# Down projection of a SwiGLU encoder: two feature chunks per PSUM bank instead of one

## Chip, cores, metric

One NeuronCore of one Trainium2 chip; the seven others do nothing. The metric is device time in microseconds (us) of one execution of the whole kernel. Inputs, outputs and weights lie in HBM in fp32.

## What is computed

Two requests, 1024 and 512 tokens of width 1024, go through the same trunk of two layers. Layer 0 mixes tokens with a Fourier transform, layer 1 with grouped-query attention; after each mixer stands a dense SwiGLU block, whose third product is what the change touches.

```python
D_MODEL, DEPTH, SEQ, DEC_SEQ = 1024, 2, 1024, 512
D_FF = 2816                                     # 22 chunks of 128 features

def swiglu_ffn(x, g, w_gate, w_up, w_down):
    h = rms_norm(x, g)
    return (jax.nn.silu(h @ w_gate) * (h @ w_up)) @ w_down

def run_trunk(x):
    for i in range(DEPTH):
        x = x + (fourier_mixer(...) if i % 2 == 0 else attention_mixer(...))
        x = x + swiglu_ffn(x, norm_ffn[i], ffn_w_gate[i], ffn_w_up[i], ffn_w_down[i])
    return x
```

## The kernel before

Activations are kept with features on the 128 partitions and tokens along the free dimension, in blocks of 512 tokens: block 0 is the short request, blocks 1 and 2 the long one. A width of 1024 is eight chunks (`NC = 8`), the hidden width is 22 chunks (`NF = 22`). Every fp32 operand is split into a high part in `float32r` and a low remainder (`split`: ScalarE copies the high part, VectorE or GpSimd subtracts), and one fp32 product is three matmuls high·high, high·low, low·high with 512 columns, issued by `mm3` (lines 255, 256, 257). "Product" below means one such group of three.

**Two kinds of SwiGLU block.** `ffn` handles block 0 alone. For each hidden chunk `fc` it runs eight products into the gate bank and eight into the up bank (`part`), then SiLU (line 804), the multiplication by up (805), and the split into the tile `mid`; in layer 0 both banks are first multiplied by a row factor (802, 803). `ffn_pair` handles blocks 1 and 2 together, two hidden chunks `f0`, `f1` per pass, by seven steps named B11, B21, T2, T1, B22, T3, N4 in place of eight (a Strassen–Winograd scheme). A step is four quarters `j` of two products each, into two banks; `times` runs it. The stationary operand of a step is put together by `stationary` (ScalarE copy at line 248, GpSimd subtraction at 249, twice each), after GpSimd sums of raw weights in `operands` (lines 966 to 972). The moving operands come from HBM (tiles `ring`) or stay in SBUF (`op`, `late`). A pass yields four `mid` tiles, one for each block and hidden chunk: after B21 (block 1, f0), B22 (block 2, f0), T3 (block 2, f1) and N4 (block 1, f1).

**Down.** Each `mid` tile is multiplied with eight 128x128 pieces of the down weights, one for each output chunk `dc`. Each of these products has a PSUM bank of its own out of two (`bank()`, tag `cF`), and VectorE adds the bank to the fp32 accumulator `acc[dc]` (line 762 in `ffn`, line 900 in `ffn_pair`). So each hidden chunk of each block costs eight products and eight additions.

**What sets the order.** Down products don't follow their `mid` tile at once. They are put on a list `pend`, and taken from it one at a time between the gate and up products: `one()` in `ffn`, at gate chunk 5, 6, 7 and after each up chunk; `some()` in `ffn_pair`, after every one of the 56 products of a pass, with a credit of 0.62. Main stages and side stages (Fourier mixer of the long request, attention, output projections) are generators that `weave` takes turns with, by the costs that they yield and the fixed costs `FFN_US`, `PAIR_US` and so on. The program's scheduler then assigns buffers and may bring an instruction forward on its queue when its buffer is free. SyncE issues the weight loads.

**Buffers.** `weights(src)` loads one 128x1024 piece into one of two `raw` tiles by one DMA, ScalarE copies the high part (line 286) and GpSimd subtracts (line 287) into one of four `w` tiles (tag `wF`). Gate, up, down and the steps' stationary operands all take their `w` tile from these four. There are two `mid` tiles.

The order of the stages: Fourier mixer of block 0; `ffn(0, 0)` woven with the long request's Fourier mixer and with `moving`, which makes the moving operands of the first pair on VectorE (lines 831 to 858); the pair of layer 0 woven with attention of block 0; `ffn(1, 0)` woven with attention of blocks 1 and 2 and with `moving` for the second pair; the pair of layer 1, alone from about 2450 us on.

Of the kernel before, what the change touches and what calls it, by code (L numbers as in the profile page):

```python
# [11 lines left out]
F32R = mybir.dt.float32r  # L12
# [113 lines left out]
def trunk_kernel(ctx: ExitStack, tc: tile.TileContext, t: dict):  # L126
# [18 lines left out]
    for name, kw in (("sbH", {}), ("sbF", {}), ("sbX", {}), ("psF", PS), ("psX", PS)):  # L145
# [10 lines left out]
    }  # L156
    uid = [0]

# [113 lines left out]
    def after(dst, src):  # L272

        dve.tensor_copy(dst[0:1, 0:1], src[0:1, 0:1])

    def weights(src):

        return list(weights_by(src))[-1]

    def weights_by(src):  # L280
        raw = raw_tile(D)
        sp.dma_start(raw, src)
        w = w_tile(2, NC, P)
        yield w
        flat = w.rearrange("p h c n -> p h (c n)")
        pinned(act.copy(flat[:, 0], raw)) if early else act.copy(flat[:, 0], raw)  # L286
        pool.tensor_tensor(flat[:, 1], raw, flat[:, 0].bitcast(F32), op=ALU.subtract)  # L287
        yield w
# [389 lines left out]
    def mixer_projection(seq, done):  # L678
# [8 lines left out]
        for n in range(NC):  # L687
            if two:
                for m in range(len(ws), min(n + 2, NC)):
                    ws.append(weights(cwd[m // 4][:, m % 4].rearrange("p k j c -> p (k j c)")))  # L690
                w = ws[n].rearrange("p h (k j) c -> p h k j c", k=2)
                wv = lambda b, k, j: w[:, b, k, j]
            else:
                wv = lambda b, k, j: turned[n // 4 * 4 + j][:, b, k, n % 4 * P : (n % 4 + 1) * P]
                if n >= 5:
                    early.append(weights_by((t["gate"], t["up"], t["down"])[n - 5][0, 0]))
                    first[n - 5] = next(early[-1])
                if n >= 6:
                    next(early[n - 6])
# [50 lines left out]
    def ffn(layer, b, h, out=None):  # L750
        h = h()
        here = b in resident
        acc = resident.pop(b) if here else accumulators()
        kept[b] = acc
        yield 0.0

        def down(m, wd, fc, dc):
            ps = bank()
            mm3(ps, wd[:, 0, dc], wd[:, 1, dc], m[:, 0], m[:, 1], True, True)
            if fc == 0 and not here:  # L760
                sp.dma_start(acc[dc], xres[b][:, dc, :])
            dve.tensor_tensor(acc[dc], ps, acc[dc], op=ALU.add)  # L762
            if fc == NF - 1:
                new_residual(b, dc, acc[dc], None if out is None else out[:, dc, :])

        def one():
            if pend:
                pend.pop(0)()

        ready = {(v, 0): first[i] for i, v in enumerate(("gate", "up", "down"))} if here else {}  # L770

        def want(v, fc):
            if fc < NF and (v, fc) not in ready:
                ready[v, fc] = weights(t[v][layer, fc])

        for fc in range(NF):
            want("gate", fc)
            want("up", fc)
            want("gate", fc + 1)
            wg, wu = ready.pop(("gate", fc)), ready.pop(("up", fc))  # L780
            ga, up = bankg(), bankg()
            for dc in range(NC):
                part(wg, h, ga, dc)
                if here and fc == 0:
                    part(wu, h, up, dc)
                if dc >= 5:
                    one()
                if dc % 2:
                    yield 1.4 if dc < 5 else 2.4
            want("down", fc)  # L790
            wd = ready.pop(("down", fc))
            for dc in range(NC):
                if dc == 4:
                    want("up", fc + 1)
                if not (here and fc == 0):
                    part(wu, h, up, dc)
                one()
                if dc % 2:
                    yield 2.4 if dc < 5 else 1.8
# [8 lines left out]
            pend.extend(lambda dc=dc, m=m, wd=wd, fc=fc: down(m, wd, fc, dc) for dc in range(NC))  # L808

# [52 lines left out]
    def ffn_pair(layer, blocks, ring, places, wide, outs):  # L862
# [28 lines left out]

        credit = [0.0]

        def down(m, wd, fc, b, dc):
            ps = bank()
            mm3(ps, wd[:, 0, dc], wd[:, 1, dc], m[:, 0], m[:, 1], True, True)
            acc = accs[b][dc]
            if fc == 0:
                sp.dma_start(acc, xres[b][:, dc, :])
            dve.tensor_tensor(acc, ps, acc, op=ALU.add)  # L900
            if fc == NF - 1:
                new_residual(b, dc, acc, None if outs is None else outs[b][:, dc, :], room=spare)
# [21 lines left out]

        turn = [0]

        def times(w, name, f0):

            turn[0] += 1
            if turn[0] % (3 if wide else 2) == 0:  # L930
# [4 lines left out]
            for j in range(4):  # L935
# [4 lines left out]
                    some()  # L940
                if not at_hand:
                    fetch()
                yield 2.2
            return list(enumerate(banks))

        def hidden(up, s, fc, b, wd):
            dve.tensor_tensor(up, up, s, op=ALU.mult)
            m = tl("mid", [2, TB], F32R, "mid")
            split(m[:, 0], m[:, 1], up)
            pend.extend(lambda dc=dc: down(m, wd, fc, b, dc) for dc in range(NC))  # L950

        def silu(s, x):
            act.activation(s, x, AF.Silu)
# [27 lines left out]
        ready = [next(ahead_)]  # L981
        yield 15.0

        def step(x):
            w = ready.pop()
            ready.append(next(ahead_))
            return (yield from times(w, x, f0))

        U, V, W = (tmp(), tmp()), (tmp(), tl("ss", [TB], F32, "ssF")), tl("W", [TB], F32, "WT", raws)
        for f0 in range(0, NF, 2):  # L990
            f1 = f0 + 1
            for i, ps in (yield from step("B11")):
                act.copy(U[i], ps)
            wd0 = weights(t["down"][layer, f0])
            for i, ps in (yield from step("B21")):
                plus(ps, ps, U[i])
                if i == 0:
                    s = silu(V[0], ps)
                else:
                    hidden(ps, s, f0, blocks[0], wd0)  # L1000
            for i, ps in (yield from step("T2")):
                plus(U[i], ps, U[i])
            for i, ps in (yield from step("T1")):
                plus(V[i], ps, U[i])
            for i, ps in (yield from step("B22")):
# [1 line left out]
                if i == 0:  # L1007
                    s = silu(W, ps)
                else:
                    hidden(ps, s, f0, blocks[1], wd0)  # L1010
            wd1 = weights(t["down"][layer, f1])
            for i, ps in (yield from step("T3")):
                plus(U[i], ps, U[i])
                plus(ps, ps, V[i])
                if i == 0:
                    s = silu(V[0], ps)
                else:
                    hidden(ps, s, f1, blocks[1], wd1)
            for i, ps in (yield from step("N4")):
                plus(ps, ps, U[i])  # L1020
                if i == 0:
                    s = silu(U[0], ps)
                else:
                    hidden(ps, s, f1, blocks[0], wd1)
        while pend:
            pend.pop(0)()
        close_pool("gT")
# [403 lines left out]
```

## Time and profile before

| | |
|---|---|
| median of 3 runs | 3070.05 us (3065.45 to 3073.8) |
| the profiled execution | 3078.82 us |
| its span, first to last instruction | 3077.0 us |
| mean granted TensorE clock | 0.979 |
| busy: TensorE / VectorE / GpSimd / ScalarE | 96% / 59% / 43% / 40% |
| additions of down (lines 900 and 762) | 704 and 352 |

Times in the profile are from the span's start. PE is TensorE's matmul queue, PEld its weight loads, DVE VectorE, ACT ScalarE, POOL GpSimd, SP SyncE. In a table by windows "x220" is the number of instructions; PEclk is the granted clock as a share of full speed. In a list of waits, "PE c L255 <- DVE acc L762: 11.6, 10, 3.4" reads: matmuls of line 255 that write a tile `c` sat idle for 11.6 us in all, 10 times, at most 3.4 us, until line 762 on VectorE, which writes `acc`, let them go. PE's busy time is modelled from pipelined matmuls, so that a window that is wholly busy may still have room.

### The profile page before, as it was taken

The numbers are of one execution on the slowest core, as the hardware profiler recorded it, in microseconds if no ns is written. First come the engines' busy times: TensorE is split into PE (matmuls) and PEld (weight loads), VectorE is DVE, ScalarE is ACT, GpSimd is POOL, SyncE is SP. The second block draws the span as 40 slices with busy tenths as digits, with TensorE's granted clock in tenths as the row PEclk, the third lists the DMA queues.
The fourth block names the chain that finished last, engine by engine and source line by source line (L and its number), as shares of the span: only waits on it lengthen the run. The fifth ranks groups of instructions, "written<-read, shape, count | busy, mean of one in ns | idle before, by whom it ended". The sixth has DMA issues, their size and how long they took to land.

```text
span 3077.0 us, 37570 instructions
## 1 busy us (share of the span) xinstructions
PE 2953.5 (96%) x13920; PEld 2415.3 (78%) x13920; DVE 1804.1 (59%) x3049; ACT 1237.4 (40%) x1929; POOL 1337.6 (43%) x746
## 2 busy tenths in 40 slices
PE   7999989989999999999899999999997999999999
PEld 6778868778888888787788788888775778888887
DVE  6785685565456666446644456565346555555566
ACT  5543232323325654223434377777433222222221
POOL 4334244545444446543343322221545555554552
PEclk8999999999999999999999999999998999999999
DMA  6435475777677778775533312211557944335332
GB/s 222 140 103 171 138 266 169 254 235 250 238 247 244 246 235 280 273 250 197 189 116 108 103 62 66 66 52 59 187 169 265 341 166 162 137 138 200 141 137 89
DMA packets 197880, 547.19 MB, mean 178 GB/s; under 512 B 21600, under 2 KB 35936, under 8 KB 197312
## 3 DMA queue, kind: packets, MB, share of 16 engines
q1 hardware_dynamic: 196768, 539.99, 51.8%
q0 software_dynamic: 640, 3.74, 0.4%
q8 instruction: 110, 1.80, 0.2%
q10 hardware_dynamic: 288, 1.05, 0.1%
q14 instruction: 74, 0.61, 0.1%
HBM read 472.34 MB, written 72.35 MB: 177 GB/s over the span
## 4 chain that ended last, share of the span: by engine, by line
PE 74%; DVE 6%; DMA 4%; POOL 3%; issue 3%; ACT 2%; SPq 0%; POOLq 0%; ACTq 0%; DVEq 0%
PE c L255 11%; PE c L256 11%; PE c L257 11%; PE a L255 6%; PE a L257 6%; PE a L256 6%; PE g L257 6%; PE g L256 6%; PE g L255 6%; PE c L1138 2%; POOL w L287 2%; DMA raw<-in_down_dram 1%; DVE col L1121 1%; DMA t<-dot 1%; POOL w L249 1%
## 5 line engine op out<-in xcount | busy, mean ns | idle before, releaser
L287 POOL TENSOR_TENSOR w<-raw,w 128x1024 fp32r<-128x1024 f32 x244 | 587.3, 2415 | 1022.8 <-ACT w L286 999.9
L900 DVE TENSOR_TENSOR acc<-c,acc 128x512 f32<-128x512 f32 x704 | 481.3, 688 | 390.9 <-PE c L257 384.3
L249 POOL TENSOR_TENSOR w<-raw,w 128x512 fp32r<-128x512 f32 (+1 forms) x332 | 437.3, 1341 | 511.7 <-ACT w L248 498.1
L255 PE MATMUL c<-mid,w 128*128 128x512 f32 x1056 | 424.8, 406 | 39.5 <-ACT mid L248 13.2
L257 PE MATMUL c<-mid,w 128*128 128x512 f32 x1056 | 418.4, 396 | 2.8 <-POOL w L287 2.8
L286 ACT CAST w<-raw 128x1024 fp32r<-128x1024 f32 x244 | 255.3, 1049 | 411.6 <-issue 121.5
L256 PE MATMUL c<-mid,w 128*128 128x512 f32 x1056 | 418.9, 397 | 1.1 <-DVE mid L249 0.9
L762 DVE TENSOR_TENSOR acc<-c,acc 128x512 f32<-128x512 f32 x352 | 239.9, 686 | 195.1 <-PE c L257 191.6
L248 ACT CAST w<-raw 128x512 fp32r<-128x512 f32 (+1 forms) x332 | 197.3, 635 | 388.1 <-PE a L257 158.2
L257 PE MATMUL g<-h,w 128*128 128x512 f32 x704 | 282.7, 402 | 5.8 <-POOL w L287 5.8
L255 PEld LDWEIGHTS c<-mid,w 128*128 128x128 f32 x1056 | 198.9, 190 | 113.9 <-DVE acc L900 28.8
L255 PE MATMUL g<-h,w 128*128 128x512 f32 x704 | 282.9, 402 | 5.5 <-ACT t L804 4.8
L256 PE MATMUL g<-h,w 128*128 128x512 f32 x704 | 281.7, 400 | 1.8 <-DVE h L252 1.8
L257 PEld LDWEIGHTS c<-mid,w 128*128 128x128 f32 x1056 | 201.2, 191 | 45.1 <-POOL w L287 4.1
L256 PEld LDWEIGHTS c<-mid,w 128*128 128x128 f32 x1056 | 201.5, 191 | 42.0 <-DVE mid L249 5.1
L255 PE MATMUL a<-ring,w 128*128 128x512 f32 x488 | 193.7, 397 | 6.1 <-DVE x L831 4.2
L256 PE MATMUL c<-h,w 128*128 128x512 f32 x480 | 190.5, 397 | 6.3 <-POOL h L249 5.4
L257 PE MATMUL a<-ring,w 128*128 128x512 f32 x488 | 192.4, 394 | 3.0 <-POOL w L249 2.9
L255 PE MATMUL c<-h,w 128*128 128x512 f32 x480 | 190.2, 398 | 3.2 <-ACT h L251 3.2
L256 PE MATMUL a<-ring,w 128*128 128x512 f32 x488 | 192.0, 393 | 0.0
L257 PE MATMUL c<-h,w 128*128 128x512 f32 x480 | 189.0, 394 | 0.0
L255 PEld LDWEIGHTS g<-h,w 128*128 128x128 f32 x704 | 135.9, 193 | 36.2 <-ACT t L804 6.6
(368 smaller groups left out, 5958.6 us busy)
## 6 DMA issues: line engine op xcount, KB each, us to landing
ring<-mov_B SPq DMA_DIRECT2D x204, 512.0 KB, 5.1
ring<-mov_T SPq DMA_DIRECT2D x176, 512.0 KB, 5.6
raw<-in_down_dram SPq DMA_DIRECT2D x88, 512.0 KB, 3.7
raw<-in_gate_dram SPq DMA_DIRECT2D x44, 512.0 KB, 3.6
raw<-in_up_dram SPq DMA_DIRECT2D x44, 512.0 KB, 3.6
raw<-in_gate_dram SPq DMA_DIRECT2D x88, 256.0 KB, 4.5
raw<-in_up_dram SPq DMA_DIRECT2D x88, 256.0 KB, 5.6
ring<-mov_N SPq DMA_DIRECT2D x44, 512.0 KB, 5.4
```

Of the source, the lines that this page charges most:

```text
L248: act.copy(hi, src)
L249: eng.tensor_tensor(lo, src, hi.bitcast(F32), op=ALU.subtract)
L255: pe.matmul(out, lh, rh, start=first, stop=False)
L256: pe.matmul(out, lh, rl, start=False, stop=False)
L257: pe.matmul(out, ll, rh, start=False, stop=last)
L286: pinned(act.copy(flat[:, 0], raw)) if early else act.copy(flat[:, 0], raw)
L287: pool.tensor_tensor(flat[:, 1], raw, flat[:, 0].bitcast(F32), op=ALU.subtract)
L762: dve.tensor_tensor(acc[dc], ps, acc[dc], op=ALU.add)
L900: dve.tensor_tensor(acc, ps, acc, op=ALU.add)
L1121: dve.tensor_tensor(st[:, 1:2], st[:, 0:1], nrqc[:, gq, h : h + 1], op=ALU.mult)
L1138: pe.transpose(tr[:, i * P : (i + 1) * P], p[:, kc * P : (kc + 1) * P], ident)
```

## The change

Down works on pairs of hidden chunks. For each output chunk, the products of two hidden chunks go into the same PSUM bank, six matmuls in one accumulation, and VectorE adds the bank's sum to `acc[dc]` once.

In `ffn` the pair is (f0, f0+1) with f0 even. The down weights of a pair are loaded as two pieces A and B of 128x1024: A holds output chunks 0 to 3 of both hidden chunks, B chunks 4 to 7, each loaded by two DMAs of 128x512. The sixteen half-steps of a pair are listed with the first two output chunks interleaved (both first halves, then both second halves). Two of them run in the odd chunk (up chunks 6 and 7) with the `mid` that is there already, fourteen in the next even chunk, from gate chunk 3 on.

In `ffn_pair` the `mid` tiles are collected for each block (`mids`). Block 2's pair is f0 and f1 of the same pass; block 1's is f1 of the pass before and f0 of this one, so that block 1's first and last chunk stand alone. A block's sixteen half-steps are put on the list inside a step, by a hook: for block 1 after quarter 2 of T2, for block 2 after quarter 0 of N4. The down weights are fetched by hooks after quarter 2 of B21 and of T3. The credit is 0.85 with a cap of 1.7. A third `mid` tile (tag `m2`) is added.

```diff
+    def down_src(layer, f0, half):
+        return [t["down"][layer, f0 + i, :, half * TB : (half + 1) * TB] for i in range(2)]
...
     def weights_by(src):
         raw = raw_tile(D)
-        sp.dma_start(raw, src)
+        srcs = src if isinstance(src, list) else [src]
+        n = D // len(srcs)
+        for i, v in enumerate(srcs):
+            sp.dma_start(raw[:, i * n : (i + 1) * n], v)
...
@@ ffn
+        def halves(ms, wds, f0, dc):
+            box = []
+            def half(i):
+                w = wds[dc // 4].rearrange("p h (f c) n -> p h f c n", f=2)
+                mm3(box[0], w[:, 0, i, dc % 4], w[:, 1, i, dc % 4], ms[i][:, 0], ms[i][:, 1], i == 0, i == 1)
+            def begin():
+                box.append(bank())
+                if f0 == 0 and not here:
+                    sp.dma_start(acc[dc], xres[b][:, dc, :])
+                half(0)
+            def end():
+                half(1)
+                dve.tensor_tensor(acc[dc], box[0], acc[dc], op=ALU.add)
+                if f0 + 2 == NF:
+                    new_residual(b, dc, acc[dc], None if out is None else out[:, dc, :])
+            return begin, end
...
+        def open_items(ms, f0):
+            wds = [ready.pop(("A", f0))]
+            pairs = [halves(ms, wds, f0, dc) for dc in range(NC)]
+            turns = [pairs[0][0], pairs[1][0], pairs[0][1], pairs[1][1]]
+            for v in pairs[2:]:
+                turns.extend(v)
+            pend.extend(turns)
+            return wds
...
         for fc in range(NF):
-            want("gate", fc)
-            want("up", fc)
-            want("gate", fc + 1)
+            f0, odd_ = fc - fc % 2, fc % 2
             wg, wu = ready.pop(("gate", fc)), ready.pop(("up", fc))
+            if not odd_ and wds is not None:
+                want("B", f0 - 2)
+                wds.append(ready.pop(("B", f0 - 2)))
             for dc in range(NC):
+                if odd_ and dc == 4:
+                    want("A", f0)
                 part(wg, h, ga, dc)
-                if dc >= 5:
+                if not odd_ and dc >= 3:
                     one()
                 if dc % 2:
-                    yield 1.4 if dc < 5 else 2.4
+                    yield 1.36 if odd_ or dc < 3 else 2.0 if dc == 3 else 2.7
...
             for dc in range(NC):
...
-                one()
+                if not odd_:
+                    one(2 if dc == 3 else 1)
+                elif dc >= 6:
+                    one()
...
@@ ffn_pair
-        def down(m, wd, fc, b, dc):
-            ps = bank()
-            mm3(ps, wd[:, 0, dc], wd[:, 1, dc], m[:, 0], m[:, 1], True, True)
...
-            dve.tensor_tensor(acc, ps, acc, op=ALU.add)
+        def down(b, parts, dc, begins, ends):
+            box, acc = [], accs[b][dc]
+            def half(k):
+                m, wd = parts[k]
+                if k == 0:
+                    box.append(bank())
+                    if begins:
+                        sp.dma_start(acc, xres[b][:, dc, :])
+                mm3(box[0], wd[:, 0, dc], wd[:, 1, dc], m[:, 0], m[:, 1], k == 0, k + 1 == len(parts))
+                if k + 1 == len(parts):
+                    dve.tensor_tensor(acc, box[0], acc, op=ALU.add)
+                    if ends:
+                        new_residual(b, dc, acc, None if outs is None else outs[b][:, dc, :], room=spare)
+            return [lambda k=k: half(k) for k in range(len(parts))]
...
+        def downs(b, begins=False, ends=False):
+            parts, mids[b] = mids[b], []
+            lists = [down(b, parts, dc, begins, ends) for dc in range(NC)]
+            for k in range(len(parts)):
+                pend.extend([lists[0][k], lists[1][k]])
+            for v in lists[2:]:
+                pend.extend(v)
         def some():
-            credit[0] += 0.62
+            credit[0] = min(credit[0] + 0.85, 1.7)
...
-            wd0 = weights(t["down"][layer, f0])
-            for i, ps in (yield from step("B21")):
+            for i, ps in (yield from step("B21", lambda: fetch_down(f0), 2)):
...
-            for i, ps in (yield from step("T2")):
+            for i, ps in (yield from step("T2", lambda: downs(blocks[0], begins=f0 == 0), 2)):
...
-            wd1 = weights(t["down"][layer, f1])
-            for i, ps in (yield from step("T3")):
+            for i, ps in (yield from step("T3", lambda: fetch_down(f1), 2)):
...
-            for i, ps in (yield from step("N4")):
+            for i, ps in (yield from step("N4", lambda: downs(blocks[1], begins=f0 == 0, ends=f0 + 2 == NF), 0)):
...
+        downs(blocks[0], ends=True)
         while pend:
             pend.pop(0)()
```

More of the change, by code (lines that the diff above doesn't have):

```diff
@@ L772, in want, with one @@
+        def one(n=1):
+            for _ in range(n):
+                if pend:
+                    pend.pop(0)()
+        ready = {v: first[i] for i, v in enumerate((("gate", 0), ("up", 0), ("gate", 1)))} if here else {}
         def want(v, fc):
             if fc < NF and (v, fc) not in ready:
-                ready[v, fc] = weights(t[v][layer, fc])
+                ready[v, fc] = weights(down_src(layer, fc, "AB".index(v)) if v in "AB" else t[v][layer, fc])
+        def open_items(ms, f0):
[6 more added lines that the diff above has]
+            return wds
@@ L807, in ffn @@
             split(m[:, 0], m[:, 1], up)
-            pend.extend(lambda dc=dc, m=m, wd=wd, fc=fc: down(m, wd, fc, dc) for dc in range(NC))
+            if odd_:
+                ms.append(m)
+            else:
+                ms = [m]
+        want("B", NF - 2)
+        wds.append(ready.pop(("B", NF - 2)))
     def moving(blocks, gain, out, ring, helped):
@@ L892, in ffn_pair @@
         credit = [0.0]
-        def down(m, wd, fc, b, dc):
[L895 to L902, printed above, removed]
+        def down(b, parts, dc, begins, ends):
[12 more added lines that the diff above has]
+            return [lambda k=k: half(k) for k in range(len(parts))]
+        mids, nmid = {b: [] for b in blocks}, [2]
+        def downs(b, begins=False, ends=False):
[5 more added lines that the diff above has]
+                pend.extend(v)
         def some():
-            credit[0] += 0.62
+            credit[0] = min(credit[0] + 0.85, 1.7)
             while credit[0] >= 1.0:
@@ L925, in ffn_pair, with times @@
         turn = [0]
-        def times(w, name, f0):
+        def times(w, name, f0, hook, at):
             turn[0] += 1
@@ L942, in times, with hidden @@
                     fetch()
+                if hook and j == at:
+                    hook()
                 yield 2.2
             return list(enumerate(banks))
-        def hidden(up, s, fc, b, wd):
+        def hidden(up, s, b, wd):
             dve.tensor_tensor(up, up, s, op=ALU.mult)
-            m = tl("mid", [2, TB], F32R, "mid")
+            nmid[0] += 1
+            m = tl("mid", [2, TB], F32R, "mid") if nmid[0] % 3 else tl("mid", [2, TB], F32R, "m2", raws)
             split(m[:, 0], m[:, 1], up)
-            pend.extend(lambda dc=dc: down(m, wd, fc, b, dc) for dc in range(NC))
+            mids[b].append((m, wd))
         def silu(s, x):
@@ L982, in ffn_pair, with step, fetch_down @@
         yield 15.0
-        def step(x):
+        def step(x, hook=None, at=0):
             w = ready.pop()
             ready.append(next(ahead_))
-            return (yield from times(w, x, f0))
+            return (yield from times(w, x, f0, hook, at))
+        wds = {}
+        def fetch_down(fc):
+            wds[fc] = weights(t["down"][layer, fc])
         U, V, W = (tmp(), tmp()), (tmp(), tl("ss", [TB], F32, "ssF")), tl("W", [TB], F32, "WT", raws)
```

34 lines of the change are left out of this document (15 added, 19 removed), and 2 rows, old and new, of the table BUFS.

## The prediction, made before the changed kernel ran

> **What bounds the kernel now.** I read the page first, then windows by stage, the waits of TensorE, the groups of lines, and timelines of single stalls.
>
> ```profile
> span 3077.0 us, 37570 instructions
> ...
> PE 2953.5 (96%) x13920; PEld 2415.3 (78%) x13920; DVE 1804.1 (59%) x3049; ACT 1237.4 (40%) x1929; POOL 1337.6 (43%) x746
> ...
> L900 DVE TENSOR_TENSOR acc<-c,acc 128x512 f32<-128x512 f32 x704 | 481.3, 688 | 390.9 <-PE c L257 384.3
> ...
> L762 DVE TENSOR_TENSOR acc<-c,acc 128x512 f32<-128x512 f32 x352 | 239.9, 686 | 195.1 <-PE c L257 191.6
> ```
>
> TensorE is the bound, and the change leaves all its matmuls in place. VectorE has slack on average, so an addition saved is worth something only where VectorE is full for a while. The windows say where:
>
> ```profile
> core 0: us, PE busy (x) PEld busy (x) DVE busy (x) ACT busy (x) POOL busy (x), PEclk, DMA share, GB/s
> 350.00:450.00 100.00, 90.31 (x425) 72.82 (x424) 83.53 (x139) 37.08 (x57) 44.45 (x22) 1.00 0.64 224
> 450.00:500.00 50.00, 46.72 (x189) 37.03 (x189) 31.65 (x42) 16.16 (x21) 22.78 (x12) 0.93 0.61 211
> 600.00:700.00 100.00, 87.60 (x352) 68.50 (x350) 62.18 (x82) 29.89 (x48) 44.24 (x25) 0.90 0.77 260
> 700.00:950.00 250.00, 249.40 (x1138) 205.41 (x1137) 133.61 (x243) 79.14 (x130) 116.74 (x70) 1.00 0.73 248
> 1200.00:1300.00 100.00, 93.22 (x394) 75.44 (x393) 49.67 (x76) 30.89 (x51) 66.98 (x41) 0.97 0.82 287
> 2290.00:2400.00 110.00, 90.89 (x356) 69.89 (x356) 70.99 (x97) 38.04 (x61) 67.12 (x38) 0.89 0.69 250
> 2500.00:3050.00 550.00, 549.99 (x2407) 449.36 (x2406) 327.35 (x493) 140.15 (x236) 290.47 (x182) 1.00 0.41 145
> ```
>
> From 2500 to 3050, where the second pair runs alone, TensorE is busy for 549.99 of 550 us at full clock: nothing is to be won there, and a product of three matmuls costs 3 x 550/2407 = 0.69 us. Losses sit at the seams of the stages: 350 to 500, 600 to 700, 1200 to 1300, 2290 to 2400. These four hold 9.7 + 3.3 + 12.4 + 6.8 + 19.1 = 51 us of idle TensorE. Who ended its waits, over the whole span:
>
> ```profile
> PE c L255 <- ACT mid L248: 13.2, 8, 2.6
> PE c L255 <- DVE acc L900: 12.0, 12, 3.2
> PE c L255 <- DVE acc L762: 11.6, 10, 3.4
> PE a L255 <- ACT p L1124: 8.3, 6, 1.6
> PE a L257 <- POOL w L249: 7.3, 6, 2.6
> PE g L257 <- POOL w L287: 5.8, 3, 2.4
> ```
>
> Down heads this list: 23.6 us for a bank that VectorE had not emptied, 13.2 us for `mid`. One stall from close by, VectorE first, then TensorE:
>
> ```profile
> 384.12 1.27 DVE L762 TENSOR_TENSOR acc<-c,acc 128x512 f32<-128x512 f32 x2
> 385.32 2.36 DVE L249 TENSOR_TENSOR l<-x,l 128x512 fp32r<-128x512 f32 x1
> 387.60 1.27 DVE L762 TENSOR_TENSOR acc<-c,acc 128x512 f32<-128x512 f32 x2
> ...
> 388.34 0.50 PE L255 MATMUL c<-mid,w 128*128 128x512 f32 x1 [0.96 <-DVE acc L762]
> ```
>
> A 2.36 us subtraction of `moving` stands between two pairs of additions. Both banks are full, and the next product waits.
>
> **The change part by part.**
>
> *Additions removed.* `ffn`: 352 become 2 layers x 11 pairs x 8 = 176. `ffn_pair`: block 1 has 10 pairs and two single chunks, 12 x 8 = 96, block 2 has 88; two layers make 368 in place of 704. So 512 additions x 0.687 us = 352 us leave VectorE, a fifth of its 1804 us. Almost all of it lies beside a busy TensorE and is worth nothing by itself.
>
> *Waits for a bank.* A bank is now filled by six matmuls (1.37 us) and emptied by one addition, so VectorE may be late by 0.69 us more before TensorE notices, and has half the additions. The waits last up to 3.4 us, so the long ones only shorten. Bounds 0 and 23.6 us; I take two thirds, **16 us gained**.
>
> *Waits for `mid`.* ScalarE's copy in the second pair:
>
> ```profile
> L248 ACT CAST mid<-a 128x512 fp32r<-128x512 f32 x24 | 14.1, 587 | 41.6 <-DVE a L947 41.6
> ```
>
> In `ffn` the tile of the odd chunk is first needed after four gate products in place of six, 1.4 us sooner, but only at every second chunk, and VectorE's queue ahead of it is shorter. Before the change a down product could ask for its tile 22 times a layer, now it is pressed 11 times. Bounds: 13 us gained, 13 us lost. In `ffn_pair` the new close call is block 2: T3's tile is needed by the third half-step of N4, after five step products and two half-steps, 7 x 0.69 = 4.8 us. Its chain is five additions or products of 0.69 on VectorE, begun about when T3 ends, and ScalarE's copy of 0.59, 4.0 us to the high part: just covered; without that cover it costs what VectorE is late by. I take **3 us gained** in all.
>
> *The clock.* Windows with idle TensorE show a lower clock. Lost in them: 0.07 x 50 + 0.10 x 100 + 0.03 x 100 + 0.11 x 110 = 28.6 us. Close to one stall:
>
> ```profile
> 440.00:459.00 19.00, 16.56 (x72) 13.06 (x70) 16.33 (x21) 6.65 (x9) 10.20 (x5) 1.00 0.72 253
> 459.00:466.00 7.00, 6.39 (x14) 4.66 (x15) 5.02 (x9) 1.87 (x4) 0.00 (x0) 0.52 0.95 356
> ...
> PE c L255 <- ACT mid L248: 4.7, 2, 2.6
> ```
>
> The wait list is that of 440 to 470 us: two waits of 2.6 and 2.1 us, and after them 7 us at about half clock, so a stall of 2 us can cost 3.5 us more. Down's waits are about a third of those in the four stretches, so I take a third of 28.6, **9 us gained**; bounds 0 and 28.6. The Trainium skill, page "TensorE: Matmul & The Clock Gate", Part 1, says that the clock halves after an idle window of about 3.4 us, and that the window runs free of the kernel. By that rule alone hardly a wait of down's here (the longest has 3.4 us) would halve the clock by itself, this term would be near 0 and the sum 9 us smaller; the row above, with waits of 2.6 us at most, speaks for more.
>
> *Less crowding in `moving`.* From 2290 to 2400 its VectorE chain competes with 35 additions:
>
> ```profile
> L762 DVE TENSOR_TENSOR acc<-c,acc 128x512 f32<-128x512 f32 x35 | 23.6, 686 | 28.8 <-PE c L257 28.8
> ```
>
> Half of them, 12 us of VectorE, goes. I count it at 0, because the waits that it ends are in the terms above; up to 10 us more is possible.
>
> *The last products.* At the end stand 11 half-steps of block 2 and 8 single products of block 1, in place of 3 and 8. In 3056 to 3077 the additions (0.69 us each) hold up products of the same length:
>
> ```profile
> L255 PEld LDWEIGHTS c<-mid,w 128*128 128x128 f32 x16 | 3.0, 187 | 5.4 <-DVE acc L900 5.1 <-issue 0.2
> ```
>
> Block 2's half-steps now cover the chain of the last `mid` tile, and bring one addition for two products. **2 us gained**, bounds 0 and 5.
>
> *Loads of down.* Issue, landing and the two halves of the split, from timeline, page and the groups of the second pair:
>
> ```profile
> 2704.14 0.33 SPq L282 DMA_DIRECT2D raw<-in_down_dram  x1
> ...
> raw<-in_down_dram SPq DMA_DIRECT2D x88, 512.0 KB, 3.7
> ...
> L286 ACT CAST w<-raw 128x1024 fp32r<-128x1024 f32 x18 | 19.0, 1055 | 83.6 <-issue 70.3 <-POOL raw L969 13.2
> ...
> L287 POOL TENSOR_TENSOR w<-raw,w 128x1024 fp32r<-128x1024 f32 x18 | 43.1, 2395 | 48.1 <-ACT w L286 48.1
> ```
>
> In `ffn` each piece comes by two DMAs: 44 more issues on SyncE, 0.33 us each, 15 us of a queue that mostly waits. In `ffn_pair` the fetches move from before B21 and T3 into these steps, past ring loads of SyncE and stationary splits of ScalarE and GpSimd, half a step to one step later; the first use moves later too, from the start of T2 to the start of T1. The landing of 3.7 us and the splits (1.05 and 2.40 us) make 7.2 us; from the hook to the half-step that needs the piece are 13 products, 8.9 us. Covered by 1.7 us, cost 0; if that cover goes, up to 2 us in each of 44 places.
>
> *Weight tiles in `ffn_pair`.* This is what speaks most against the change. A down piece serves two blocks and is now held from B21 to the next pass's B21, or from T3 to the next T3, nearly seven steps in place of about four. Of four `w` tiles two are always down's, so one stationary operand is in use and only one can be made ahead. From T3 after its first quarter to N4's first, and from late B21 to T2's third quarter, no half-step fills in: T3 is about 9 products, 6.2 us. In it the next stationary operand must be made, after the copy of `mid` that stands ahead on ScalarE:
>
> ```profile
> L249 POOL TENSOR_TENSOR w<-raw,w 128x512 fp32r<-128x512 f32 x128 | 162.7, 1295 | 169.2 <-ACT w L248 169.2
> ...
> L248 ACT CAST w<-raw 128x512 fp32r<-128x512 f32 x127 | 72.7, 620 | 202.1 <-PE a L257 98.9 <-PE c L257 51.4 <-PE g L257 28.4
> ```
>
> The `mid` copy ends about 3.2 us into the step; a ScalarE copy (0.6) and two GpSimd subtractions (2 x 1.3) end at 6.4 us; TensorE wants the second half at about 6.2 + 1.1 = 7.3 us. Room of 0.9 us, against over 2 us before, when the step had 13 products. In these 550 us the stationary copies already wait 202 us for a tile to come free. I charge **5 us lost**, for the woven pair, where side work shares both queues; bounds 0 and 66 (the rival below).
>
> *Sum.* 16 + 3 + 9 + 2 - 5 = 25 us gained. The profiled execution took 3078.8 us, 8.8 us above the median of 3070.05, so 3054 by its own time, and 3045 as a median; I say **3046**. A difference under 0.3%, 9 us, can't be told from none.
>
> **The rivals.**
>
> *A, slower: the second tile for looking ahead is missed.* If GpSimd takes a down split (2.40 us) ahead of a stationary operand in the thin steps T2 and T3, the operand ends at 8.8 us in place of 6.4, 1.5 us after TensorE wants it. Two steps x 11 passes x 2 layers x 1.5 = 66 us lost, less 30 gained: about 3106. It decides from 30/44 = 0.7 us a step. For it: the 202 us above, and 2500 to 3050 has only room for loss. Against it: GpSimd is idle there for half the time (290 of 550 us), and the down piece's tile comes free about a microsecond after the stationary one's, so that the latter is first in line.
>
> *B, no change.* The additions come off a queue that isn't the bound. The same 2.4 us subtractions still stand ahead of `mid` and of the remaining additions, and the waits go by another name: 5 us for banks plus 3 for the clock, given back by `mid` in `ffn` and by the weight tiles. About 3068. For it: 700 to 950, with 53% of VectorE in use, loses only 0.6 us.
>
> *C, gains in full.* All 23.6 us for banks, half of `mid`'s 13.2, half of the clock's 28.6, 5 at the end, 5 in `moving`, nothing lost: 54 us, 3016. For it: the stalls are where VectorE is full, 84% over 350 to 450.
>
> **How the numbers follow.** My forecast, 3030 to 3061, 0.47; C, under 3030, 0.11; B, within 9 us of 3070, 0.22; A, above 3079, 0.20. Faster is the first and C, 0.58; same 0.22; slower 0.20. The range runs from 3020, which leaves out half of C, to 3085, which takes in A's small prices and leaves out its larger ones, together under 2 in 10.
>
> **What would show it.** Right: 176 and 368 additions; 1452 us of VectorE; waits of `c` L255 for `acc` near 8 us in all; clock above 0.90 in 600 to 700 and 0.89 in the stretch before the second pair; the pair alone still without idle TensorE. Wrong: new waits of `a` or `g` matmuls for `w` at L249 or L248 in the second pair (A); waits for `mid` L248 above 20 us in `ffn`; or the bank waits unchanged, because the long subtractions and not the additions' number made them.

## The result, and the profile after

| | before | changed |
|---|---|---|
| median of 4 runs | 3070.9 us (3065.45 to 3073.8) | 3039.24 us (3033.61 to 3041.51) |
| profiled execution, span | 3078.82, 3077.0 us | 3038.65, 3036.9 us |
| granted clock | 0.979 | 0.985 |

The ratio is 0.9896, with a 95% interval of 0.9877 to 0.9916: 31.7 us saved. The forecast was 3046, in a range of 3020 to 3085. The profiled execution of before was a slow one, 8.8 us above the median of 3070.05 and with a granted clock of 0.979, where 54 later executions of the same kernel, on three chips, had 0.981 to 0.986 (median 0.983). So the two traces are 40 us apart, and some 8 of these are not the change's. From the page after, in the same form as before:

```profile
span 3036.9 us, 37132 instructions
...
PE 2925.5 (96%) x13920; PEld 2407.4 (79%) x13920; DVE 1487.2 (49%) x2537; ACT 1235.8 (41%) x1931; POOL 1338.7 (44%) x746
...
L954 DVE TENSOR_TENSOR acc<-c,acc 128x512 f32<-128x512 f32 x368 | 253.1, 689 | 410.7 <-PE c L257 402.9
...
L780 DVE TENSOR_TENSOR acc<-c,acc 128x512 f32<-128x512 f32 x176 | 120.5, 687 | 130.8 <-PE c L257 128.5
...
raw<-in_down_dram SPq DMA_DIRECT2D x88, 256.0 KB, 3.1
...
raw<-in_down_dram SPq DMA_DIRECT2D x44, 512.0 KB, 5.2
```

The additions are 368 and 176, as counted beforehand; VectorE fell by 317 us and TensorE's 13920 matmuls stayed. (Line 900 of before is 954 now, 762 is 780, 287 is 294, 286 is 293, 804 is 847, 1124 is 1198.) Who ended TensorE's waits, over the whole span:

```profile
PE a L255 <- ACT p L1198: 9.3, 8, 2.0
PE c L255 <- ACT mid L248: 9.0, 6, 4.2
...
PE c L255 <- DVE acc L780: 5.1, 5, 1.8
PE g L255 <- ACT w L293: 4.9, 2, 4.0
...
PE c L257 <- POOL w L294: 4.0, 5, 1.2
...
PE c L256 <- DVE mid L249: 3.5, 3, 3.1
PE c L255 <- DVE acc L954: 3.0, 2, 1.7
```

Waits for a bank fell from 23.6 to 5.1 + 3.0 = 8.1 us, and the longest from 3.4 to 1.8. All waits together fell by less: TensorE's idle time went from 3077.0 - 2953.5 = 123.5 to 3036.9 - 2925.5 = 111.4 us, so some waits elsewhere grew. The windows of before, the last one shifted by 40 us because that stage begins earlier now:

```profile
core 0: us, PE busy (x) PEld busy (x) DVE busy (x) ACT busy (x) POOL busy (x), PEclk, DMA share, GB/s
350.00:450.00 100.00, 90.60 (x375) 72.25 (x374) 72.76 (x102) 38.68 (x57) 47.04 (x23) 0.93 0.75 258
450.00:500.00 50.00, 48.85 (x215) 39.79 (x214) 16.44 (x24) 14.47 (x18) 28.25 (x13) 1.00 0.53 173
600.00:700.00 100.00, 94.19 (x405) 74.93 (x404) 49.16 (x74) 31.26 (x50) 53.13 (x30) 0.97 0.78 270
700.00:950.00 250.00, 247.88 (x1147) 205.29 (x1146) 108.95 (x202) 87.42 (x144) 115.76 (x70) 1.00 0.72 243
1200.00:1300.00 100.00, 98.49 (x433) 80.84 (x432) 36.28 (x54) 27.43 (x44) 56.99 (x35) 1.00 0.84 298
2290.00:2400.00 110.00, 94.80 (x383) 74.64 (x383) 55.72 (x67) 33.25 (x51) 67.77 (x40) 0.92 0.81 292
2460.00:3010.00 550.00, 550.00 (x2426) 454.73 (x2425) 235.81 (x351) 141.93 (x239) 293.55 (x183) 1.00 0.42 145
```

The seams do better (600 to 700: 405 matmuls in place of 352, clock 0.97 in place of 0.90), but a window at a fixed time can hold other work than before, so the gain by stage is better taken from the times at which equal amounts of TensorE's work (columns passed through its matmuls) were done. The second column is a second execution of the changed kernel (the last run under "The load in one part only"), 33 us shorter than this one of before:

| stretch (by the times of before) | gained, us | second execution, us |
|---|---|---|
| start to 500 | +17 (9 of them in the first 120 us) | +11 (4) |
| 560 to 700, start of the woven first pair | +11 | +12 |
| 700 to 1200, the woven first pair | -4 | -5 |
| 1200 to 1300 | +8 | +9 |
| 1350 to 1549, end of the pair and start of `ffn(1, 0)` | +5 | +4 |
| 1549 to 2296, `ffn(1, 0)` beside attention | -20 | -19 |
| 2296 to 2480, seam to the second pair | +18 | +16 |
| 2480 to 3056, the second pair alone | +4 | +4 |
| the last products | +2 | +2 |

The rows don't add up exactly because the stretches leave small gaps and are rounded. The first row holds what differs between executions: 6 us lie between the two columns, and they are of one and the same kernel. The seams give more than the total, and one stage that the prediction did not look at takes some back. These are the windows of that stage with equal numbers of matmuls; first the row of before, then that of the changed kernel with what its TensorE waited for in the stage:

```profile
1549.00:2296.00 747.00, 727.01 (x3838) 602.73 (x3838) 377.10 (x696) 428.11 (x614) 237.25 (x108) 0.99 0.31 97
```

```profile
1513.00:2279.00 766.00, 734.88 (x3835) 605.31 (x3834) 357.23 (x636) 433.22 (x622) 242.03 (x111) 0.98 0.31 99
...
PE a L255 <- ACT w L248: 3.6, 2, 2.0
PE c L256 <- DVE mid L249: 3.1, 1, 3.1
PE c L256 <- DVE h L252: 2.0, 1, 2.0
```

19 us longer, 11 of them idle TensorE and 8 more busy time at a lower clock. The waits are scattered over attention and `ffn`: no single one carries it. But the numbers are equal and the work is not: the trace has 744 matmuls of gate and up in the second window and 707 in the first, 358 of down and 380. How much the stage loses depends on where its end is set. Ended 6 us earlier (1549 to 2290 against 1513 to 2266, 3805 and 3806 matmuls) it is 753 us against 741, 12 us. From the first gate product of `ffn(1, 0)` to its last, seam included, the work is the same but for three down products, and the windows are

```profile
1443.00:2394.00 951.00, 900.72 (x4531) 737.61 (x4532) 511.83 (x889) 507.68 (x733) 337.40 (x159) 0.97 0.37 123
```

```profile
1407.00:2361.00 954.00, 899.88 (x4523) 736.14 (x4522) 471.12 (x798) 510.72 (x735) 336.38 (x157) 0.97 0.37 121
```

so the whole stage became 3 us longer, 5 with the three missing products of 0.69 us. Most of the -20 and of the +18 is the same time on two sides of one boundary.

What is left of the stalls near 440 us, from the timeline of the changed kernel (start, duration, engine; in brackets the wait before it) and two windows around it:

```profile
434.22 2.23 DVE L906 TENSOR_TENSOR x<-x 128x512 f32<-128x512 f32 x1
436.37 0.69 DVE L848 TENSOR_TENSOR g<-g,t 128x512 f32<-128x512 f32 x1
...
436.97 1.28 DVE L249 TENSOR_TENSOR l<-x,l 128x512 fp32r<-128x512 f32 x2
437.09 0.58 ACT L248 CAST mid<-g 128x512 fp32r<-128x512 f32 x1
...
437.73 0.79 PE L255 MATMUL c<-mid,w 128*128 128x512 f32 x1 [4.16 <-ACT mid L248]
...
430.00:437.00 7.00, 3.57 (x16) 2.63 (x14) 7.00 (x9) 2.96 (x5) 3.65 (x2) 0.95 0.83 310
437.00:444.00 7.00, 6.27 (x16) 4.96 (x17) 3.23 (x6) 0.67 (x2) 0.00 (x0) 0.56 0.91 312
```

VectorE is busy for 7.00 of 7 us, almost all of it with `moving` (line 906 last), before it has done the multiplication of line 848, from which `mid` is copied. The 7 us from 437 on run at 0.56 of the full clock: by this row the stall of 4.2 us costs about 3 more (7.00 x 0.44, an estimate). Halved additions don't help here, since what stands ahead is not an addition.

### The profile page after: what moved, and what is told of

It is laid out like the page before. It is cut to its first block, busy times and chain, and to the rows that moved or that the text cites. A ratio compares the mean times of both kernels' runs of the same rounds, so it can differ in the third digit from the quotient of the medians.

```text
span 3036.9 us, 37132 instructions
## 1 busy us (share of the span) xinstructions
PE 2925.5 (96%) x13920; PEld 2407.4 (79%) x13920; DVE 1487.2 (49%) x2537; ACT 1235.8 (41%) x1931; POOL 1338.7 (44%) x746
## 5 line engine op out<-in xcount | busy, mean ns | idle before, releaser
L954 DVE TENSOR_TENSOR acc<-c,acc 128x512 f32<-128x512 f32 x368 | 253.1, 689 | 410.7 <-PE c L257 402.9
L293 ACT CAST w<-raw 128x1024 fp32r<-128x1024 f32 x244 | 254.9, 1049 | 319.0 <-PE c L257 111.4
L780 DVE TENSOR_TENSOR acc<-c,acc 128x512 f32<-128x512 f32 x176 | 120.5, 687 | 130.8 <-PE c L257 128.5
```

Of the source, the lines that this page charges most:

```text
L780: dve.tensor_tensor(acc[dc], box[0], acc[dc], op=ALU.add)
L954: dve.tensor_tensor(acc, box[0], acc, op=ALU.add)
```

## Experiments

Three accounts of the 31.7 us were set against each other. **Load**: 512 additions fewer on VectorE, so that `moving` and `mid` come sooner. **Hand-over**: a bank changes hands half as often and takes six matmuls to fill, whatever VectorE does otherwise. **Order**: the new places of half-steps, loads, the credit and the third `mid` tile do it, and the additions don't matter. Each ratio is to runs of the kernel before on the same chip.

### The order alone

Everything of the change stays, but each half-step gets its own bank and its own addition again, 1056 in all. The same edit is made in `ffn_pair`.

```diff
             def half(i):
                 w = wds[dc // 4].rearrange("p h (f c) n -> p h f c n", f=2)
-                mm3(box[0], ..., i == 0, i == 1)
+                ps = bank()
+                mm3(ps, ..., True, True)
+                dve.tensor_tensor(acc[dc], ps, acc[dc], op=ALU.add)
```

> The changed kernel's order, loads, list of half-steps, credit and third mid tile, but every half-step fills a bank of its own and is added by itself: 1056 additions again. Theory 1 (it is the additions, by VectorE's load or by the bank's hand-over): back to 3058 to 3080, waits of c L255 for acc above 18 us. Theory 2 (it is the new order of down's products and loads, the additions are beside the path): at or below 3048, waits for acc below 12 us.

Measured 3069.68 us, ratio 1.0011 (0.9999 to 1.0023). Its waits:

```profile
PE c L255 <- ACT mid L248: 16.4, 7, 3.6
...
PE c L255 <- DVE acc L952: 10.6, 9, 4.1
PE c L255 <- DVE acc L772: 9.2, 10, 2.2
```

Bank waits are back at 19.8 us and the gain is gone, so the order by itself brings nothing and the pairing is needed. It does one thing that the prediction had excluded. Over the second pair alone, before and this run:

```profile
2480.00:3000.00 520.00, 519.99 (x2277) 425.03 (x2276) 308.90 (x464) 133.10 (x223) 277.39 (x174) 1.00 0.44 156
```

```profile
2480.00:3000.00 520.00, 520.00 (x2295) 429.96 (x2294) 315.07 (x472) 134.48 (x227) 281.62 (x175) 1.00 0.45 153
```

18 matmuls more in 520 us (4 us) though VectorE has as many additions as before. In before, down's first matmuls (line 255) started 235 ns after their predecessor on average in the pair alone and its second ones (line 256) 231 ns, in the changed kernel and in this run 226 to 227 ns, like nearly all others: before, about a tenth of the first ones were held for a moment that is too short for the list of waits. The new order removes that; what it wins here it loses elsewhere.

### VectorE's load given back

The changed kernel, with an idle reduction of `acc` behind each of the 512 paired additions. It writes into a small tile of its own that nobody reads, and holds no bank.

```diff
                 dve.tensor_tensor(acc[dc], box[0], acc[dc], op=ALU.add)
+                dve.tensor_reduce(cols.tile([P, 1], F32, tag="load", name=nm("load")), acc[dc], op=ALU.max, axis=AX.X)
```

> The changed kernel with its 544 additions and six-matmul banks, and 512 reductions of an accumulator (128x512, SBUF) on VectorE behind the additions of paired chunks, whose results nobody reads: VectorE's load is given back, the hand-over of banks is not. Theory 1a (VectorE's load in its full stretches): 3055 to 3075, VectorE busy about 1800 us. Theory 1b (the bank is handed over half as often, whatever VectorE does): 3036 to 3048. Theory 2: 3036 to 3048 too.

Measured 3063.33 us, ratio 0.9986 (0.9975 to 0.9997), 5.5 us under the kernel before on that chip (3068.81): 26 of the 31.7 us are gone. The page shows the load as meant, and the waits how little of it reaches the banks (8.4 + 3.4 = 11.8 us):

```profile
PE 2938.0 (96%) x13920; PEld 2406.0 (79%) x13920; DVE 1808.5 (59%) x3049; ACT 1233.7 (40%) x1929; POOL 1339.7 (44%) x746
...
L957 DVE TENSOR_REDUCE load<-acc 128x1 f32<-128x512 f32 x336 | 228.8, 682 | 7.3
...
PE c L255 <- ACT mid L248: 13.0, 8, 3.4
...
PE c L255 <- DVE acc L780: 8.4, 6, 3.1
PE g L255 <- DVE mid L249: 4.4, 3, 3.4
...
PE c L255 <- DVE acc L955: 3.4, 5, 1.0
```

So the two waits go apart. For a bank: 23.6 us before, 19.8 with the order alone, 11.8 here, where VectorE has as much to do as before, 8.1 in the changed kernel. Most of what the banks gained stays without any relief of VectorE, and that part is the hand-over's. For `mid` (lines 248 and 249 together): 14.1 us before, 18.1 here, 12.7 in the changed kernel; there the load counts.

By its time alone this run would make VectorE's load four fifths of the gain, as the expectation for load had it (3055 to 3075). Two later kernels, with the reductions in one part only, showed that it can't be taken so.

### The load in one part only

```diff
-                    if len(parts) == 2:
+                    if len(parts) == 2 and not wide:      # all but the second pair: 344 reductions
...
+                    if len(parts) == 2 and wide:          # the second pair alone: 168, none in ffn
```

> As the run with 512 idle reductions, but without the 168 in the second paired block, which runs alone: 344 reductions, all in stages that are woven with others. In the second pair the reductions made every matmul a little longer without any wait. Theory 1a (VectorE's load where it is full costs the time): 3052 to 3060. Rival (a good part of the loss was that longer matmul in the second pair): 3040 to 3049.

> The changed kernel with the 168 idle reductions in the second paired block alone, where VectorE was not full and TensorE never waited. If VectorE's load costs only where it is full: within 2 us of the changed kernel. If the reductions' reads of SBUF lengthen the matmuls there: 4 to 6 us slower than it, without new waits in the list.

Measured: without the second pair 3065.96 us, 0.9985 (0.9974 to 0.9995); in the second pair alone 3053.74 us, 0.9947 (0.9935 to 0.996), against 3037.2 us, 0.9889 (0.9873 to 0.9904), for the changed kernel itself, which ran along:

> The changed kernel once more, on the chip of the other three: 3034 to 3043, ratio to the kernel before 0.988 to 0.992.

Neither kernel came out as expected, by load or by its rival. The second pair's reductions should have cost at most 6 us, but that kernel is 16.5 us slower; for the one without them 3060 was the highest time expected, and it is 3065.96. The expectations took the longer matmuls of the second pair for an effect of the reductions that run there. The windows say otherwise. First the changed kernel, then the kernel whose second pair holds no reductions at all:

```profile
2500.00:2950.00 450.00, 450.00 (x1985) 371.98 (x1985) 190.72 (x283) 113.64 (x191) 234.69 (x147) 1.00 0.45 161
```

```profile
2500.00:2950.00 450.00, 450.00 (x1970) 369.05 (x1970) 190.99 (x283) 115.81 (x195) 241.18 (x151) 1.00 0.45 160
```

VectorE's work is the same, 191 us in 283 instructions, TensorE is busy throughout at full clock, and still 15 matmuls fewer are done: 228.4 ns each in place of 226.7. Over the whole trace, the mean distance of successive 512-column matmuls that follow each other closely (some 10390, under 260 ns apart) is 229.1 ns in all three kernels with reductions, and 227.7 ns in the changed kernel (both executions), the one with only `ffn_pair` paired and the one with later half-steps. The difference is 1.4 ns x 10390 = 14.7 us, present also where no reduction runs. (In the kernel before the mean is 227.8 ns, so the 31.7 us themselves don't come from this.) It isn't every matmul, as mean durations in the same window show, first for the changed kernel, then for the one without reductions there:

```profile
L255 PE MATMUL a<-ring,w 128*128 128x512 f32 x125 | 48.6, 389 | 0.0
...
L255 PE MATMUL a<-op,w 128*128 128x512 f32 x88 | 34.2, 389 | 0.0
```

```profile
L255 PE MATMUL a<-ring,w 128*128 128x512 f32 x128 | 49.8, 389 | 0.0
...
L255 PE MATMUL a<-op,w 128*128 128x512 f32 x72 | 28.2, 392 | 0.0
```

With `ring` as the moving operand nothing changed, with `op` each takes longer; by the starts it is 232 in place of 227 ns to the next matmul. What the three kernels share is one more tag in the pool `cols`, four buffers of 128x1. That it is this tile isn't shown, as no kernel has it without reductions. But some 14.7 us of the loss don't depend on whether a reduction runs beside. Taken off, the load given back costs 26 - 15 = 11 us of the 31.7 with all reductions, and 28.8 - 14.7 = 14 us (3065.96 against 3037.2) without those of the second pair; idle TensorE agrees, with 3059.5 - 2938.0 = 121.5 us in the first of these runs against 111.4 in the changed kernel. As the order gives nothing, some 18 to 21 us are left for the hand-over of banks and what follows from it. No run isolates that part without an added tile, and the parts need not add up, so the shares stay estimates.

### One kind of block only

`ffn` paired and `ffn_pair` as before (with three `mid` tiles and a credit of 0.9 for the first 16 slots), and the other way round.

```diff
-        def halves(ms, wds, f0, dc):           # in the second kernel
+        def down(m, wd, fc, dc):
...
-        def downs(b, begins=False, ends=False): # in the first kernel
+        def down(m, wd, fc, b, dc):
```

> Only the block alone (ffn) in pairs of hidden chunks; the paired block as before, but with three mid tiles and, for the sixteen first places of its list, a credit of 0.9, so that the longer rest of ffn's list is gone in time. Theory 1: the stretches where VectorE is full are those of ffn beside the moving operands, so most of the gain, 15 to 25 us, is here: 3046 to 3056. Theory 2: no part can be told in advance. Rival: the gain is the paired block's: above 3060.

> Only the paired block in pairs of hidden chunks, the block alone as before. Theory 1: 8 to 15 us of gain, from the seam at 600 to 700, from 1200 to 1300 and from the pair alone: 3056 to 3063. Rival (the paired block carries the gain): 3045 or less. Rival A of the prediction (weight tiles held longer cost something that the other half hides): above 3071.

Measured 3057.76 us, 0.9965 (0.9951 to 0.9979), and 3055.47 us, 0.9962 (0.9947 to 0.9977): 11 and 13 us under the kernel before on that chip (3068.81), each just outside of what was expected for it (3046 to 3056, and 3056 to 3063). Their sum is 24 us of the 31.7. Both kinds of block pay, though the second pair alone, which has half of `ffn_pair`'s additions, gains only 4 us by the trace, which the order alone gave there too: the pairs' gain is where they start and where other work is woven in.

### Fewer long subtractions on VectorE

The kernel before, and then the changed one, with the low parts of B22, T3 and N4 of the first pair's moving operands subtracted on GpSimd in place of VectorE. This asks whether the load of `moving` alone, with down as it is, would bring the gain of the first seam.

```diff
-        yield from paired(0, OPERANDS[:2], {}, False, None)
+        yield from paired(0, ("B11", "B21", "B22", "T3", "N4"), {}, False, None)
```

> The kernel before, but the subtractions for B22, T3 and N4 of the first pair's moving operands (12 of 128x512) go from VectorE to GpSimd. It unloads VectorE in the stretch 350 to 450 alone, without touching down. Theory 1a (VectorE's load in its full stretches costs the time): 4 to 12 us faster than before, waits for acc L762 in that stretch below half. Rival (the load matters only through the additions' own place in the queue): within 3 us of before.

> The changed kernel with the same 12 subtractions on GpSimd. Theory 1a: VectorE is less full there already, so less is left to win: 2 to 6 us faster than the changed kernel, 3033 to 3037. Rival: GpSimd is shared with the weights of ffn, so its splits come later and nothing or less than nothing is won: 3039 or more.

Measured 3069.41 us, 0.9995 (0.9985 to 1.0005), on the kernel before, and 3037.61 us, 0.9896 (0.9882 to 0.9909), on the changed one (3039.24 and 3037.2 without it): nothing; for the kernel before that was the rival's case. From the groups of the first, 350 to 500:

```profile
L762 DVE TENSOR_TENSOR acc<-c,acc 128x512 f32<-128x512 f32 x57 | 39.1, 688 | 20.7 <-PE c L257 20.6
L255 PE MATMUL c<-mid,w 128*128 128x512 f32 x58 | 24.1, 416 | 11.0 <-ACT mid L248 7.3 <-DVE acc L762 3.7
...
L249 POOL TENSOR_TENSOR l<-x,l 128x512 fp32r<-128x512 f32 x12 | 19.2, 1606 | 7.3 <-ACT l L248 7.3
...
L249 DVE TENSOR_TENSOR l<-x,l 128x512 fp32r<-128x512 f32 x8 | 11.0, 1376 | 0.1
```

Twelve subtractions, 1.23 us each on VectorE in this stretch before, left it; the other eight take 1.38 us. TensorE still waits 11.0 us for `mid` and banks here (4.1 + 7.0 us before). VectorE's subtractions there took 24.5 us before and take 11.0; its busy time in the stretch falls by less, from 115.2 to 106.7 us. So VectorE is relieved by some 8 us close to the stalls, and the stalls stay. That speaks, like the waits above, for the hand-over and against load alone; how a larger relief would do isn't shown.

### Half-steps later in the even chunk

The changed kernel; in `ffn` the first half-step of an even chunk comes after gate chunk 4 in place of 3, and two are taken after up chunks 3 and 5. The aim was the 9.0 us of waiting for `mid`.

```diff
-                if not odd_ and dc >= 3:
+                if not odd_ and dc >= 4:
                     one()
...
-                    one(2 if dc == 3 else 1)
+                    one(2 if dc in (3, 5) else 1)
```

The costs that `ffn` yields are adapted to it. A second kernel adds the edit for GpSimd; the first was run once more, beside the changed kernel's second run.

> The changed kernel, but in ffn the even chunk's first half-step comes after gate chunk 4 in place of 3 (and two after up chunks 3 and 5), so that the odd chunk's mid tile has one product more of time. If the shorter lead for mid costs something in ffn: waits for mid L248 fall from 9.0 to below 6 us, and 2 to 6 us are won, 3033 to 3037. Rival: the long waits for mid come from single long VectorE instructions ahead of its chain, so that 0.7 us of lead changes nothing: within 3 us of 3039.

> Both of the last two edits on the changed kernel. Theory 1a with both effects: 3028 to 3035. Rival: one of them does nothing, then the time of the other.

> The changed kernel with the later first half-step in ffn once more, beside the changed kernel. If its gain is real: 6 to 12 us below the changed kernel of this call. Rival (the earlier run caught a fast execution): within 4 us of it.

Measured 3028.99 us, 0.9869 (0.985 to 0.9889); with GpSimd's share 3035.38 us, 0.9881 (0.9867 to 0.9894); again 3033.16 us, 0.9878 (0.9862 to 0.9894). The reason given for it fails: in the first of these runs the waits for `mid` are 11.1 us, not below 9.0. What fell is the stage that the change had made longer (the row is of the stage, the waits are of the whole span):

```profile
1512.00:2261.00 749.00, 726.30 (x3837) 602.27 (x3836) 342.02 (x633) 433.11 (x621) 239.92 (x110) 0.99 0.31 99
...
PE c L255 <- ACT mid L248: 11.1, 7, 3.4
PE c L255 <- DVE acc L780: 8.1, 6, 2.8
```

749 us for as many matmuls, in place of 766, and 752 in the repetition; the changed kernel took 766 in both of its profiled executions. From the first gate product of `ffn(1, 0)` to its last, where the work is the same, it is 944 and 948 us in place of 954 and 955. So 7 to 10 us of that stage are a matter of how the half-steps and the yielded costs fit `weave`; some of it is lost again in the seam to the second pair, where a gate product waits 5.6 us for the low part of `mid`. The edit moved the half-steps and the costs at once, so which of the two did it stays open. As a whole this is the fastest version that ran, but its intervals overlap with the changed kernel's, which it beat by 4 us where both ran side by side: 6 to 12 were expected of a real gain, so a gain of the whole kernel isn't shown. With the GpSimd edit on top, which had no effect on either kernel, its median was 6 us higher: between schedules that differ in places far apart, 5 to 10 us can't be put down to the edit.

## Why the prediction was right, and where not

**Waits for a bank**: 16 us forecast, bounds 0 and 23.6; measured 23.6 - 8.1 = 15.5 us. A second execution has 8.0. The reasoning (a bank lasts 0.69 us longer, half the additions) holds: the order alone left 19.8 us, and 11.8 were left with VectorE's load given back.

**Waits for `mid`**: 3 us forecast. Line 248 fell from 13.2 to 9.0, but the low part (line 249) rose from 0.9 to 3.5: 1.6 us net, and none in the second execution (10.1 + 3.9). The half-step that comes sooner in `ffn` meets a `mid` that is no sooner, as at 437 us.

**The clock**: 9 us forecast. Span times the share of the clock that is missing is 3077.0 x 0.021 = 64.6 us before and 3036.9 x 0.015 = 45.6 after, 19 us apart. But the profile of before is of an execution with a lower clock than any of the 54 later ones. By medians (0.983 of these 54, 0.9855 of the eight executions of the changed kernel) it is 52 against 44 us, a gain of about 8; the rounding of the clock to three places alone is worth 1.5 us, so this is an estimate. The term was about right, partly by luck: the third was taken of a loss of 28.6 us that belongs to that one execution, and of four windows alone, without the losses in the first 120 us and at 1450 to 1560. The Trainium skill's rule in "TensorE: Matmul & The Clock Gate", Part 1, under which the term would be near 0, fits the wait of 4.2 us above with the 7 us at 0.56 behind it. It does not by itself explain the stretch of before with waits of at most 2.6 us; the measured term, about 8 us and not near 0, is what the rows had spoken for.

**The last products**: 2 us forecast, about 2 measured. **Weight tiles**: 5 us charged to the woven pair, and 4 to 5 us were lost there from 700 to 1200. The waits that grew there are those of attention's products for their own operands (made at lines 248 and 249), from 0.6 to 3.8 us; side work on the two queues was part of the reason given, but that weight tiles held longer caused it isn't shown. The row that rival A needed is absent: the pair alone is busy for 550.00 of 550 us, and no wait for `w` appears in it. GpSimd's idle half does cover the thinner steps. **Loads of down** at 0: waits for the low parts of weights (line 294) are 4.0 + 3.8 us, against 2.8 + 5.8 before. The high parts of gate weights (line 293) are waited for 4.9 us in `g`, against 0.7, up to 4.0 at once, in the seam before the second pair; whether the 44 more DMAs of down have to do with it isn't shown.

**Two steps failed.** "Nothing is to be won there" from 2500 to 3050 was wrong by 4 us: a TensorE that is busy 549.99 of 550 us still did 2277 matmuls in the 520 us from 2480 where 2294 fit, because busy time includes short holds. This was not the pair alone. Busy time less the missing clock, an estimate of the work at full clock, is 2953.5 - 64.6 = 2889 us before and 2925.5 - 45.6 = 2880 after (2875 in the second execution): 9 to 14 us for the same 13920 matmuls, for which the sum had no term. And a stage was left out: `ffn(1, 0)` beside attention was taken as untouched, and as a whole it lost 3 to 5 us to the new pattern of half-steps, 12 to 19 in its body.

So the sum of 25 us, against 31.7 measured, came about in another way than forecast. Down's waits fell by 17 us (19 forecast for banks and `mid`), but idle time as a whole by 12 (9 in the second execution): other waits grew by 5 to 6, about what was charged to the weight tiles, though not in that place alone. The clock gave about 8 (9 forecast), and the short holds 9 to 14, for which there was no term. The mechanism for the banks was right; that the total came so near has some luck in it.

**The signs.** 544 additions, bank waits near 8 us (8.1), clock above 0.90 in 600 to 700 (0.97) and above 0.89 before the second pair (0.92), and the pair alone without idle TensorE all came as listed. VectorE went to 1487 us in place of 1452: the additions took 348 us away, and other operations on it grew longer by 31. None of the three signs of a wrong prediction appeared in the pair alone or in `ffn`; where the second pair begins, from 2290 to 2480, the waits of `a` matmuls for `w` of line 249 are 3.6 us, against 2.0 before.

## What to carry to other kernels

Where a PSUM bank is emptied by an addition that takes as long as its matmuls, let one bank collect two products: it helped this TensorE-bound kernel by 1%, although VectorE had 41% of its time free. After such a change look at every stage in which the touched loop shares the engines, including those that had no waits, and compare times for equal work, not windows at equal times: between the same two events of the program, since equal numbers of matmuls can be other work. Look at the clock of the execution that was profiled before taking a term from it. Count matmuls per window as well as busy time, for a TensorE that is 100% busy can still be 0.7% slow.

## What was not expected of the hardware

- **The pace of matmuls differs between kernels in a stage where nothing else does.** 226.7 and 228.4 ns a matmul in the second pair at full clock, with the same instructions on VectorE; some 15 us over a span. It is in matmuls that read `op`, among others, and not in those that read `ring`. The slower kernels have one more small tile in SBUF. Whether it is where the other tiles lie then, or something else, the traces can't tell, as they hold no addresses. For experiments: an extra tile may not be free, and a kernel with the tile alone belongs beside it.
- **VectorE and GpSimd stretch each other.** Between 350 and 500 us a subtraction with both operands in SBUF takes 1.23 to 1.38 us on VectorE in the mean, where the fastest takes 0.68, and the twelve on GpSimd take 1.61 where others of the same shape take 1.30 us; additions with one operand in PSUM stay at 0.69 us. The Trainium skill, "GPSIMD Engine Reference", section 1, says that GpSimd shares its SBUF interfaces with VectorE and contends with instructions that have two SBUF inputs. These rows agree, and it may be why moving twelve subtractions from one to the other bought nothing.
